# Moving the MLP input and the low weights of narrow pieces to other SBUF remainders

## The chip, the cores and the metric

The kernel runs on one core of one Trainium2 chip. The metric is the device time of one execution in microseconds (us); the kernel before takes 1369.39 us (median of 3 runs, 1369.24 to 1369.44).

## The reference, cut to what matters

A trunk of four decoder layers works on one sequence of 256 tokens with 1024 features in float32. Each layer adds a token mixer (retention, block-sparse attention, differential attention, retention again) and then an MLP:

```python
for i in range(DEPTH):
    h = _rmsnorm(x, norm1[i])
    x = x + mixer_i(h)
    u = relu(_rmsnorm(x, norm2[i]) @ w_up[i])      # 1024 -> 4096
    x = x + (u * u) @ w_down[i]                    # 4096 -> 1024
```

Some 237 MB of weights are read once each.

## The kernel before, in words

**Split products.** Every large product is made of float32r matmuls. An operand is split into a high part (a copy rounded to float32r, made by ScalarE) and a low part (operand minus high part, made by VectorE), and `passes` (L296 to L299) issues three matmuls into one PSUM bank: high times high (L297), high times low (L298), low times high (L299). The weight load of the next matmul runs on TensorE beside the stream of the present one.

**Weights.** `load_raw` fetches 1 MB at a time from SyncE's queue into one of three `raw` buffers. `split_piece` takes half of it and makes `whi` (L164), `split_lo` makes `wlo` (L174) and asks for the next load once both halves of a buffer are split. Six buffers of 4 KB a partition exist for each of `whi` and `wlo`, and `advance` keeps up to five pieces ahead of the one in use.

**Three shapes of piece.** A piece of `spec_a` (4 x 256 elements) is called narrow: `mm_a` uses it, with 128 columns of the weights as the stationary operand and 256 columns of the activations (`xhi`, `xlo`) as the moving one. They serve the MLP's up product (tile `up`) and retention's q and k (tile `qk`). Pieces of `spec_b` (2 x 512) and `spec_o` (1 x 1024) are wide: in `mm_b` (tiles `vg`, `qkv`) and `mm_o` (tile `acc`) the weights are the moving operand, 512 columns at a time, and the activations are the stationary one: `xhi`, `xlo` in `mm_b`; `uu` (the MLP's hidden values, high and low) or `oh`, `ol` (the mixer's output) in `mm_o`.

**What a narrow group does.** For each of 4 row blocks `passes(ps, whi, wlo, xhi, xlo)` runs. L297 moves `xhi` against `whi`, while `whi` is loaded a second time for L298. L298 moves `xlo`, while `wlo` is loaded for L299. L299 moves `xhi`, while the next `whi` is loaded for the next block's L297.

**Order.** The order of TensorE's work is written out by hand. In the MLP a step is `up(s + 1)` (two narrow pieces, 48 matmuls) and then two `out_piece` calls (24 wide matmuls); there are 16 steps in a layer. Small work (norms, softmax, transposes) is put between by `later` and `tick`.

**Normalised input.** `norm_new` allocates `xhi` and `xlo` (8 KB a partition each), once for the mixer's input and once for the MLP's input of every layer; `finish` calls it, and `norm_quarter` fills the two tiles.

**Where the tiles lie.** Pools lie one behind the other, in the order `const`, `op`, `xp`, `up`, `wp`, `mp`, `rp`. `xp` holds `xhi` and then `xlo`; `up` holds six buffers of 4 KB (`uu`, `vh`, `vl` and others); `wp` holds six `whi` and then six `wlo`. All of these sizes are multiples of 1024 bytes, so in the kernel before all of them have one remainder modulo 1024. Retention's scores `s` (high and low) lie in `mp`, behind five small tiles of three buffers padded to 32 bytes each, so they start 480 bytes off that remainder.

Of the kernel before, what the change touches and what calls it, by code (L numbers as in the profile page):

```python
# [10 lines left out]
F32R = mybir.dt.float32r  # L11
# [5 lines left out]
P = 128  # L17
S = 256
# [3 lines left out]
KC = D // P  # L22
# [9 lines left out]
def trunk(ctx, tc, x_in, rel_bias, norm1, norm2, w_up, w_down, ret_w_in, ret_w_out,  # L32
# [9 lines left out]
    xp = ctx.enter_context(tc.tile_pool(name="xp", bufs=1))  # L42
    up_ = ctx.enter_context(tc.tile_pool(name="up", bufs=1))
    wp = ctx.enter_context(tc.tile_pool(name="wp", bufs=1))
# [7 lines left out]
    NRAW, NPC = 3, 6  # L52
# [13 lines left out]
    def later(n, fn, *a):  # L66
        clock[1] += 1
        pending.append((clock[0] + n, ORDER.get(fn.__name__, 3), clock[1], fn, a))
# [10 lines left out]
    def tick():  # L79
        clock[0] += 1  # L80
        run_due()


    specs = []

    def ap2(w, off, dims):
# [62 lines left out]
    def parts(i, n):  # L149
        m = n if i else n // 2  # L150
        return [slice(c, c + m) for c in range(0, n, m)]

    def split_piece():
        i = nxt[1]
        r = i // 2
        if r >= len(specs):
            return
        nxt[1] += 1
        _, a, b = specs[r]
        half = raws[r][:, (i % 2) * (a // 2):(i % 2 + 1) * (a // 2), :]  # L160
        hi = wp.tile([P, a // 2, b], F32R, tag="hi", name="whi", bufs=NPC)
        lo = wp.tile([P, a // 2, b], F32R, tag="lo", name="wlo", bufs=NPC)
        for part in parts(i, a // 2):
            ACT.activation(hi[:, part], half[:, part], AF.Copy)  # L164
        pieces[i] = (hi, lo, half)
# [13 lines left out]
    def advance(ah=4, al=4):  # L179
        while True:  # L180
            a, b = nxt[1], nxt[3]
            if nxt[1] <= nxt[2] + ah and nxt[1] // 2 < len(specs):
                split_piece()
            if nxt[3] <= nxt[2] + al:
                split_lo()
            if (a, b) == (nxt[1], nxt[3]):
                return

    def take():
        p = pieces.pop(nxt[2])  # L190
        nxt[2] += 1
        return p
# [66 lines left out]

    st = {}  # L260

    def norm_new():
        st["hi"] = xp.tile([P, KC, S], F32R, tag="xhi", name="xhi")
        st["lo"] = xp.tile([P, KC, S], F32R, tag="xlo", name="xlo")

    def norm_quarter(l, which, c, t):
        tt = slice(t * P, (t + 1) * P)
# [65 lines left out]
    def mm_o(q, piece, src, first, last):  # L333
        c, t = q
        hi, lo = piece
        uh, ul = src
        tt = slice(t * P, (t + 1) * P)
        cc = slice(c * 512, (c + 1) * 512)
        passes(st["acc"][q], uh[:, tt], ul[:, tt], hi[:, 0, cc], lo[:, 0, cc], first, last)
# [8 lines left out]
    def finish(srcs, r2, nxt_norm):  # L348
        advance(4, 4)
        pcs = [take() for _ in srcs]  # L350
        if nxt_norm is not None:
            norm_new()
        for q in QUARTERS:
            for i, (pc, src) in enumerate(zip(pcs, srcs)):
                mm_o(q, pc, src, False, i == len(srcs) - 1)
            c, t = q
            xs = X[:, t, c * 512:(c + 1) * 512]
            ps = st["acc"][q]
            if r2 is None:
                DVE.tensor_tensor(xs, ps, xs, op=OP.add)  # L360
            else:
                DVE.scalar_tensor_tensor(xs, ps, r2[:, t:t + 1], xs, op0=OP.mult, op1=OP.add)
            if nxt_norm is None:
                nc.sync.dma_start(out.rearrange("b s d -> (b s) d")[t * P:(t + 1) * P, c * 512:(c + 1) * 512], xs)
            else:
                later(2, norm_quarter, nxt_norm[0], nxt_norm[1], c, t)
            tick()
        if nxt_norm is not None:
            later(3, rms, nxt_norm[1])


    def mlp(l):
# [21 lines left out]
        for s in range(16):  # L394
            if s + 1 < 16:
                up(s + 1)
            if not acc:
                acc_new()
                acc = True
            if s < 14:  # L400
                for m in range(2):
                    out_piece(U[s][m], s == 0 and m == 0)
                del U[s]
            elif s == 14:
                out_piece(U[s][0], False)
            else:
                finish([U[14][1]] + U[15], st["r2"], (l + 1, 0) if l + 1 < DEPTH else None)


    def retention(l):  # L410
# [107 lines left out]
        for c in range(13):  # L518
            h, i = divmod(c, 4)
            out_piece((OT[h][0][:, i, :], OT[h][1][:, i, :]), c == 0)  # L520
        finish([(OT[3][0][:, i, :], OT[3][1][:, i, :]) for i in (1, 2, 3)], None, (l, 1))


# [33 lines left out]
    def attention(l):  # L557
# [193 lines left out]
        for c in range(5):  # L751
            out_piece(srcs[c], c == 0)
        finish(srcs[5:], None, (l, 1))


    norm_new()
    for t in range(2):
        norm_quarter(0, 0, 0, t)
    split_piece()
    split_lo()  # L760
    for t in range(2):
        later(1, norm_quarter, 0, 0, 1, t)
    later(1, split_piece)
    later(1, split_lo)
    later(3, rms, 0)
# [50 lines left out]
```

## Time and profile before

| | |
|---|---|
| median of 3 runs | 1369.39 us |
| the profiled execution, its own time | 1369.67 us |
| its span, first to last instruction | 1367.9 us |
| TensorE (PE) matmul busy | 1351.8 us (99%) |
| weight loads (PEld) busy | 1188.7 us (87%) |
| VectorE (DVE), ScalarE (ACT), GpSimd (POOL) busy | 61%, 50%, 8% |
| weights' DMA queue, share of 16 engines | 51.5% |

The busy time of an engine counts overlapping instructions once. A matmul's duration is its time from start to the modelled end, longer than the distance to the next matmul's start, since matmuls are pipelined; the time of the kernel goes by the distance between starts. In the windows of one engine alone only that engine's busy time stands. In groups of lines a row reads: line, engine, operation, output and inputs, shapes and count, then busy us and the mean duration in ns, then idle time before.

### The profile page before, as it was taken

How to read it: one execution, taken by the hardware profiler on the slowest of the kernel's cores; microseconds unless marked ns; L12 is line 12 of the kernel's file. 1: busy time of each engine (PE TensorE's matmuls, PEld its weight loads, DVE VectorE, ACT ScalarE, POOL GpSimd, SP SyncE). 2: the span in 40 equal slices, each digit the busy share in tenths (PEclk: the TensorE clock that was granted, in tenths of full speed). 3: DMA queues.
4: the chain of work that ended last, by engine and by line, in shares of the span. 5: the costliest groups of instructions: out<-in, count | busy, mean ns of one | idle time of the engine just before them, and what ended most of it. 6: DMA issues, size and time to landing. Idle time of an engine off the chain costs nothing.

```text
span 1367.9 us, 19806 instructions
## 1 busy us (share of the span) xinstructions
PE 1351.8 (99%) x8020; PEld 1188.7 (87%) x8020; DVE 840.8 (61%) x1238; ACT 689.7 (50%) x1063; POOL 107.1 (8%) x314
## 2 busy tenths in 40 slices
PE   7999999999999999999999999999999999999998
PEld 7888889999987779999987789999988888899997
DVE  6766647555568856555578675555667675555554
ACT  5554436444456745444466754444454444544442
POOL 3111100000032000000021200000031011000000
PEclk9999999999999999999999999999999999999999
DMA  8545464555565346555554346555564555465551
GB/s 274 184 155 184 156 214 157 187 187 188 193 206 181 123 124 219 185 185 185 184 172 137 124 154 216 185 185 185 176 206 144 174 185 185 154 215 186 185 184 63
DMA packets 140797, 242.27 MB, mean 177 GB/s; under 512 B 4256, under 2 KB 87920, under 8 KB 140704
## 3 DMA queue, kind: packets, MB, share of 16 engines
q1 hardware_dynamic: 137872, 236.99, 51.5%
q0 software_dynamic: 1072, 2.35, 0.6%
q10 hardware_dynamic: 1760, 1.66, 0.4%
q8 instruction: 63, 1.03, 0.3%
q14 instruction: 30, 0.25, 0.1%
HBM read 239.91 MB, written 1.07 MB: 176 GB/s over the span
## 4 chain that ended last, share of the span: by engine, by line
PE 97%; ACT 1%; DMA 0%; DVE 0%; issue 0%; SPq 0%; ACTq 0%; DVEq 0%
PE acc L297 12%; PE acc L298 12%; PE acc L299 12%; PE up L299 9%; PE up L298 9%; PE up L297 9%; PE vg L297 4%; PE vg L299 4%; PE vg L298 4%; PE qkv L297 3%; PE qkv L299 3%; PE qkv L298 3%; PE qk L299 2%; PE qk L297 2%; PE qk L298 2%; PE xt L272 1%
## 5 line engine op out<-in xcount | busy, mean ns | idle before, releaser
L174 DVE TENSOR_TENSOR wlo<-raw,whi 128x1024 fp32r<-128x1024 f32 (+1 forms) x449 | 529.5, 1219 | 108.1 <-ACT whi L164 105.8
L164 ACT ACTIVATE whi<-raw 128x1024 fp32r<-128x1024 f32 (+1 forms) x449 | 451.9, 1051 | 90.8 <-PE acc L299 66.8
L297 PE MATMUL up<-xhi,whi 128*128 128x256 f32 x1024 | 290.1, 283 | 0.0
L299 PE MATMUL up<-xhi,wlo 128*128 128x256 f32 x1024 | 289.8, 283 | 0.0
L298 PE MATMUL up<-xlo,whi 128*128 128x256 f32 x1024 | 289.7, 283 | 0.0
L297 PE MATMUL acc<-whi,uu 128*128 128x512 f32 x512 | 200.5, 392 | 0.0
L298 PE MATMUL acc<-wlo,uu 128*128 128x512 f32 x512 | 199.9, 390 | 0.0
L299 PE MATMUL acc<-whi,uu 128*128 128x512 f32 x512 | 199.3, 389 | 0.0
L298 PEld LDWEIGHTS up<-xlo,whi 128*128 128x128 f32 x1024 | 196.3, 192 | 2.2
L297 PEld LDWEIGHTS up<-xhi,whi 128*128 128x128 f32 x1024 | 196.3, 192 | 2.2
L299 PEld LDWEIGHTS up<-xhi,wlo 128*128 128x128 f32 x1024 | 196.3, 192 | 0.0
L378 DVE SCALAR_TENSOR_TENSOR u<-up,u 128x512 f32<-128x512 f32 x64 | 44.2, 691 | 221.7 <-ACT u L377 221.5
L377 ACT ACTIVATE u<-up 128x512 f32<-128x512 f32 x64 | 38.1, 596 | 258.9 <-PE up L299 258.9
L299 PEld LDWEIGHTS acc<-whi,uu 128*128 128x128 f32 x512 | 96.1, 188 | 20.5
L297 PEld LDWEIGHTS acc<-whi,uu 128*128 128x128 f32 x512 | 96.4, 188 | 18.2
L298 PEld LDWEIGHTS acc<-wlo,uu 128*128 128x128 f32 x512 | 96.4, 188 | 17.6
L297 PE MATMUL vg<-whi,xhi 128*128 128x512 f32 x256 | 100.6, 393 | 0.0
L299 PE MATMUL vg<-whi,xlo 128*128 128x512 f32 x256 | 99.8, 390 | 0.0
L298 PE MATMUL vg<-wlo,xhi 128*128 128x512 f32 x256 | 99.7, 390 | 0.0
L297 PE MATMUL qkv<-whi,xhi 128*128 128x512 f32 x192 | 78.0, 406 | 0.0
L297 PE MATMUL acc<-whi,oh 128*128 128x512 f32 x192 | 76.4, 398 | 0.0
L297 PE MATMUL qk<-xhi,whi 128*128 128x256 f32 x256 | 74.0, 289 | 1.8 <-ACT whi L164 1.8
(212 smaller groups left out, 1807.7 us busy)
## 6 DMA issues: line engine op xcount, KB each, us to landing
raw<-in_w_up_dram SPq DMA_DIRECT2D x64, 1024.0 KB, 5.5
raw<-in_w_down_dram SPq DMA_DIRECT2D x64, 1024.0 KB, 5.9
raw<-in_ret_w_in_dram SPq DMA_DIRECT2D x47, 1024.0 KB, 5.2
raw<-in_ret_w_out_dram SPq DMA_DIRECT2D x16, 1024.0 KB, 4.9
raw<-in_moba_w_in_dram SPq DMA_DIRECT2D x12, 1024.0 KB, 5.2
raw<-in_diff_w_in_dram SPq DMA_DIRECT2D x12, 1024.0 KB, 5.1
raw<-in_moba_w_out_dram SPq DMA_DIRECT2D x4, 1024.0 KB, 4.8
raw<-in_diff_w_out_dram SPq DMA_DIRECT2D x4, 1024.0 KB, 4.7
```

What stands on the lines that cost most here:

```text
L164: ACT.activation(hi[:, part], half[:, part], AF.Copy)
L174: DVE.tensor_tensor(lo[:, part], half[:, part], hi[:, part].bitcast(F32), op=OP.subtract)
L272: PE.transpose(ps[:, i * P:(i + 1) * P], X[:, t, k * P:(k + 1) * P], ident)
L297: PE.matmul(ps, lhsT=ah, rhs=bh, start=first, stop=False, skip_group_check=True)
L298: PE.matmul(ps, lhsT=ah, rhs=bl, start=False, stop=False, skip_group_check=True)
L299: PE.matmul(ps, lhsT=al, rhs=bh, start=False, stop=last, skip_group_check=True)
L377: ACT.activation(u, ps, AF.Relu)
L378: DVE.scalar_tensor_tensor(u, ps, 0.0, u, op0=OP.max, op1=OP.mult)
```

## The change

Only addresses are changed. `wlo` gets a tag of its own for each of six places, padded by 128 bytes (odd places) or 384 bytes (even places), and the tile starts inside that padding or not, depending on place and shape. `xhi` and `xlo` are padded by 320 and 192 bytes, `xlo` is allocated first, and the MLP's input starts at other offsets in them than the mixer's input. Instructions, their order, shapes, DMAs and waits stay.

```diff
+    def hi_lo(i, a, b, narrow):
+        n = a * b
+        hi = wp.tile([P, n], F32R, tag="hi", name="whi", bufs=NPC)
+        odd = i % 2
+        lo = wp.tile([P, n + (32 if odd else 96)], F32R, tag="lo%d" % (i % NPC), name="wlo", bufs=1)
+        o = 0 if odd == narrow else (32 if odd else 96)
+        return (t.rearrange("p (a b) -> p a b", a=a) for t in (hi, lo[:, o:o + n]))
...
-        hi = wp.tile([P, a // 2, b], F32R, tag="hi", name="whi", bufs=NPC)
-        lo = wp.tile([P, a // 2, b], F32R, tag="lo", name="wlo", bufs=NPC)
+        hi, lo = hi_lo(i, a // 2, b, a == 8)
...
-    def norm_new():
-        st["hi"] = xp.tile([P, KC, S], F32R, tag="xhi", name="xhi")
-        st["lo"] = xp.tile([P, KC, S], F32R, tag="xlo", name="xlo")
+    def norm_new(mlp_in=False):
+
+        n = KC * S
+        lo = xp.tile([P, n + 48], F32R, tag="xlo", name="xlo")
+        hi = xp.tile([P, n + 80], F32R, tag="xhi", name="xhi")
+        oh, ol = (64, 48) if mlp_in else (80, 0)
+        st["hi"] = hi[:, oh:oh + n].rearrange("p (k s) -> p k s", k=KC)
+        st["lo"] = lo[:, ol:ol + n].rearrange("p (k s) -> p k s", k=KC)
...
-            norm_new()
+            norm_new(nxt_norm[1] == 1)
```

Worked out from these sizes, the starts in bytes, counted from the start of `whi` and modulo 1024, are:

| tile | before | after |
|---|---|---|
| `whi`, `uu`, `vh`, `vl` | 0 | 0 |
| `wlo`, narrow piece | 0 | 384 or 896 |
| `wlo`, wide piece | 0 | 0 or 512 |
| mixer input `xhi`, `xlo` | 0, 0 | 0, 512 |
| MLP input `xhi`, `xlo` | 0, 0 | 960, 704 |
| `oh`, `ol` | 0 | 512 |
| `s` | 480 | 992 |

The slices that are used within a tile begin at multiples of 512 bytes in both kernels. So modulo 512 everything that was at 0 stays there, except for the narrow `wlo` (384) and the MLP's `xhi` (448) and `xlo` (192); `s` stays at 480.

## Rows read from the trace of the kernel before

**Rows 1.** The page: busy time of engines; granted clock by slice of the span.

```profile
PE 1351.8 (99%) x8020; PEld 1188.7 (87%) x8020; DVE 840.8 (61%) x1238; ACT 689.7 (50%) x1063; POOL 107.1 (8%) x314
...
PEclk9999999999999999999999999999999999999999
```

**Rows 2.** The page: the chain that ended last, by engine.

```profile
PE 97%; ACT 1%; DMA 0%; DVE 0%; issue 0%; SPq 0%; ACTq 0%; DVEq 0%
```

**Rows 3.** Groups of lines, shapes apart: narrow and wide matmuls.

```profile
L297 PE MATMUL up<-xhi,whi 128*128 128x256 f32 x1024 | 290.1, 283 | 0.0
L299 PE MATMUL up<-xhi,wlo 128*128 128x256 f32 x1024 | 289.8, 283 | 0.0
L298 PE MATMUL up<-xlo,whi 128*128 128x256 f32 x1024 | 289.7, 283 | 0.0
...
L298 PE MATMUL acc<-wlo,uu 128*128 128x512 f32 x512 | 199.9, 390 | 0.0
...
L298 PE MATMUL qk<-xlo,whi 128*128 128x256 f32 x256 | 73.0, 285 | 0.0
```

**Rows 4.** Timeline, TensorE, one MLP step: start us, duration us, instruction.

```profile
300.27 0.40 PE L297 MATMUL acc<-whi,uu 128*128 128x512 f32 x1
...
301.43 0.39 PE L299 MATMUL acc<-whi,uu 128*128 128x512 f32 x1
...
305.51 0.39 PE L299 MATMUL acc<-whi,uu 128*128 128x512 f32 x1
305.74 0.28 PE L297 MATMUL up<-xhi,whi 128*128 128x256 f32 x1
305.85 0.28 PE L298 MATMUL up<-xlo,whi 128*128 128x256 f32 x1
...
311.37 0.28 PE L299 MATMUL up<-xhi,wlo 128*128 128x256 f32 x1
```

**Rows 5.** Tile up, 306.2 to 311.3 us: duration ns min/median/max, first and last start.

```profile
L299 PE MATMUL up<-xhi,wlo x15: 283/283/283, 306.0 to 311.0; 128*128 128x256 f32 x15
L297 PE MATMUL up<-xhi,whi x15: 283/283/283, 306.1 to 311.1; 128*128 128x256 f32 x15
```

**Rows 6.** Line L481, transposes of retention: duration ns min/median/max.

```profile
L481 PE MATMUL oT<-ident,go x64: 270/272/273, 56.8 to 1143.9; 128*128 128x128 f32 x64
```

**Rows 7.** Tile up, whole run: duration ns min/median/max.

```profile
L297 PE MATMUL up<-xhi,whi x1024: 277/283/364, 209.6 to 1352.2; 128*128 128x256 f32 x171
L298 PE MATMUL up<-xlo,whi x1024: 278/283/283, 209.8 to 1352.3; 128*128 128x256 f32 x171
```

**Rows 8.** Tiles vg and o, whole run: duration ns min/median/max.

```profile
L298 PE MATMUL vg<-wlo,xhi x256: 387/389/398, 25.6 to 1137.2; 128*128 128x512 f32 x128
...
L298 PE MATMUL o<-vl,s x24: 393/396/397, 41.0 to 1129.0; 128*128 128x512 f32 x24
```

**Rows 9.** Timeline, TensorE, retention's score product between two `vg` groups.

```profile
77.51 0.39 PE L299 MATMUL vg<-whi,xlo 128*128 128x512 f32 x1
...
78.19 0.40 PE L299 MATMUL vg<-whi,xlo 128*128 128x512 f32 x1
78.42 0.39 PE L297 MATMUL o<-vh,s 128*128 128x512 f32 x1
...
80.52 0.39 PE L297 MATMUL vg<-whi,xhi 128*128 128x512 f32 x1
...
81.20 0.39 PE L297 MATMUL vg<-whi,xhi 128*128 128x512 f32 x1
```

**Rows 10.** Groups of weight loads, shapes apart: busy us, mean ns.

```profile
L298 PEld LDWEIGHTS up<-xlo,whi 128*128 128x128 f32 x1024 | 196.3, 192 | 2.2
...
L298 PEld LDWEIGHTS acc<-wlo,uu 128*128 128x128 f32 x512 | 96.4, 188 | 17.6
```

**Rows 11.** Windows, one MLP's up phase and one narrow run: us, busy by engine; PEclk, DMA share, GB/s.

```profile
209.63:378.97 169.34, 169.34 (x1112) 155.84 (x1111) 96.65 (x102) 83.02 (x104) 1.27 (x3) 1.00 0.56 191
...
305.85:311.37 5.52, 5.52 (x48) 1.00 0.80 249
```

**Rows 12.** Waits of SyncE's queue: us in total, times, longest.

```profile
SPq L142 <- DVE wlo L174: 1172.4, 216, 16.1
```

## The prediction

> **What bounds the kernel now.** I read the page's busy times first: matmuls cover 99% of the span, VectorE 61%, ScalarE 50%, and the granted clock is at full speed, the 2.4 GHz level, in all slices [rows 1]. The chain that ended last is 97% TensorE with no DMA in it [rows 2]. So the time is the number of matmuls times the distance between their starts, and a change of addresses can matter only through that distance. Then the groups of lines: 3072 narrow matmuls belong to the MLP's up product, 1024 for each of the three passes, 283 ns each; the wide ones take some 390 ns [rows 3]. Since durations overlap, I took distances from the timeline. In a narrow run 46 distances fill the 5.52 us from 305.85 to 311.37, which is 120.0 ns each; between the wide ones 18 distances fill the 4.08 us from 301.43 to 305.51, which is 226.7 ns [rows 4].
>
> **There is something to gain in it.** At 2.4 GHz 256 columns stream in 106.7 ns and 512 in 213.3 ns. Both shapes take 13.3 ns more than that. The excess lies inside the matmul: 30 matmuls in a row lasted 283 ns to the nanosecond [rows 5], while a transpose, which also streams for 106.7 ns (128 columns of float32 in two cycles each, an estimate from its duration), lasts 272 ns [rows 6]. The difference, 11 ns, is a stretch of the stream while the next weights are loaded. Two readings tell that the stretch isn't fixed. First, the earliest narrow matmul after a wide group starts 0.11 us before the next one, not 0.12 [rows 4], and matmuls of the very same form have lasted as little as 277 or 278 ns [rows 7]. Second, an address moves it: in retention's score product the stationary operand `s` lies 480 bytes off the common remainder (32 below it modulo 512), and there the wide matmul lasts 396 ns where that of `vg` lasts 389 [rows 8]. The timeline shows it coming and going: three distances in 0.68 us before, 227 ns each; ten in 2.33 us, 233 ns each, of which nine load `s`; and three in 0.68 us again behind it [rows 9]. So remainders of the two operands that are read at once count, by +6.3 ns in the one case that can be seen.
>
> **Part by part.** The pair that counts is the stream and the weights loaded beside it. Call distance the start of the weights less that of the stream, modulo 512. Before, it is 0 in all three passes of a narrow group. After, in the MLP, L297 (moves `xhi`, loads `whi`) has 0 - 448 = 64; L298 (moves `xlo`, loads `wlo`) 384 - 192 = 192; L299 (moves `xhi`, loads the next `whi`) 64.
>
> (1) The 3072 narrow matmuls of the MLP. No row shows a distance of 64 or 192, so this is bounded. Best: the whole stretch goes, 283 to 272 [rows 5, 6], 11 ns x 3072 = 33.8 us less. Worst: they behave as `s` does, 6.3 ns more [rows 9], 19.4 us more. I take 6 ns less, from 283 to the 277 that the same form of instruction reaches in this kernel [rows 7], which is also near the distance of 0.11 us behind that short matmul [rows 4]: it is the nearest row, the same operation at another phase between stream and load, where the transposes are another operation and `s` another shape. 6 ns x 3072 = **18.4 us less**.
>
> (2) Retention's `qk`: of its 768 matmuls only the 256 of L298 change (stream at 0, weights at 384); the other two passes keep 0. Bounds as above: 256 x 11 = 2.8 us less to 256 x 6.3 = 1.6 us more; I take 0, its own row's 285 ns [rows 3], since two neighbours of three stay as they are.
>
> (3) Wide matmuls: `wlo`, `oh`, `ol` and the mixer's `xlo` shift by 0 or 512 against the rest. Slices at both steps occur before too, as every second stationary slice begins 512 bytes on, and the median stays 389 [rows 8]. Cost 0, unless modulo 512 isn't the rule (last rival).
>
> (4) The seam. Behind each narrow run five wide matmuls take 1.16 us (300.27 to 301.43) instead of 5 x 226.7 = 1133 ns [rows 4], 27 ns extra; 16 runs in each of four layers make 1.7 us. It could vanish or double; I take no change, ends 1.7 us on each side.
>
> (5) The engines that write the shifted tiles. VectorE is busy for 96.65 and ScalarE for 83.02 of the 169.34 us of an up phase [rows 11]; with 768 x 6 ns = 4.6 us less it is 59% and 50%, so slower writes stay hidden. Weights: 191 GB/s would have to become 191 x 169.34 / 164.7 = 196, and a narrow run already shows 249 [rows 11]. SyncE's queue waits 1172 us for `wlo` to free a buffer [rows 12], so loads are early, not late. No instruction, wait or DMA is added or moved. Cost 0.
>
> Sum against the profiled execution: 1369.67 - 18.4 = 1351.3 us. It lies 0.3 us above the median of 1369.39, so I forecast **1351 us**.
>
> **Rivals.** *The shift does nothing* (20%): 1369 us. For it: only an offset of 32 bytes has been seen to act, and a shift by 512 did nothing; all of the new distances are multiples of 64 bytes, so if what counts is a place within a small line, the pairs look as before. Against it: the stretch depends on phase, and a shift of 64 bytes is some 7 ns of the stream, a change of phase. The Trainium skill would have it so too: TensorE: Matmul & The Clock Gate, Part 2 (the step on LDWEIGHTS), says that TensorE reads moving operand and weights through two independent ports, so that loading the next weights takes nothing from the running matmul. By that rule no remainder matters and the sum would be 0. The trace speaks against it here: 396 ns against 389 with `s` [rows 8].
>
> *Weight loads set the pace* (12%): in the up phase they are busy for 155.84 of 169.34 us [rows 11], and a load lasts 192 ns beside narrow matmuls, 188 beside wide ones [rows 10]. If a narrow matmul cannot start until its load is through, only the 4 ns by which loads are held up come back: 4 x 3072 = 12.3 us, 1357 us. The spacing of 0.11 us speaks against it.
>
> *The new distances collide more* (18%): the stream reads two bytes where the load reads one (120 ns for 1024 bytes, beside 512 bytes of weights), so a stream that begins 64 bytes behind its weights runs into them early, where at distance 0 it starts level and leaves them behind. With the stretch of `s` on all three passes it is 19.4 us more, 1389 us; on L298 alone, 1024 x 6.3 = 6.5 us more, 1376 us. It decides as soon as the mean stretch of the three passes is over 11 ns. In it I count that the wide operands don't keep one remainder as the change says: the MLP's 1536 wide matmuls alone (512 a pass [rows 3]) x 6.3 = 9.7 us, 1379 us.
>
> **How the numbers follow.** 50% for the forecast (gains from 6 to 34 us), 12% for loads that set the pace, together 62% faster; 20% for no effect; 18% slower. About 0.2% (2.7 us) is what a measurement of this kernel can tell from no change. The range goes from the whole stretch, 1369.4 - 33.8 = 1336, to one pass in three worsened, 1376; beyond the upper end are the cases with two or three passes worsened, some 13%.
>
> **What would show it.** Right: `up` rows at 272 to 278 ns instead of 283 in all three lines, up phases of about 164.7 us instead of 169.34, wide rows at 389 and 390 as before, `s` as before. If only L298 or only L297 and L299 get shorter, one distance works and the other doesn't. The forecast is wrong if `up` stays at 283 (no effect), if loads show 188 and `up` about 279 (pace of the loads), if `up` is over 283 (collision), or if gaps of TensorE that wait for `wlo` or `raw` appear, which would say that the cover in (5) is gone.

## The result, and the profile after

The changed kernel takes 1352.09 us (median of 4 runs, 1349.88 to 1353.06) against 1369.41 us of the kernel before, a ratio of 0.9865 (95% interval 0.9853 to 0.9877): 17.3 us less, where 18.4 were forecast. Its profiled execution took 1352.26 us with a span of 1350.4 us, 17.4 and 17.5 us less than that of before.

The page's busy times and chain, and the groups of the matmuls that the terms of the sum name (the lines of `passes` are L311 to L313 now):

```profile
PE 1333.6 (99%) x8020; PEld 1170.5 (87%) x8020; DVE 840.6 (62%) x1238; ACT 689.3 (51%) x1063; POOL 106.6 (8%) x314
...
PE 97%; ACT 1%; DMA 1%; DVE 0%; issue 0%; SPq 0%; ACTq 0%; DVEq 0%
...
L311 PE MATMUL up<-xhi,whi 128*128 128x256 f32 x1024 | 283.8, 277 | 0.0
L312 PE MATMUL up<-xlo,whi 128*128 128x256 f32 x1024 | 283.5, 277 | 0.0
L313 PE MATMUL up<-xhi,wlo 128*128 128x256 f32 x1024 | 283.2, 277 | 0.0
...
L312 PE MATMUL acc<-wlo,uu 128*128 128x512 f32 x512 | 199.6, 390 | 0.0
```

```profile
L313 PEld LDWEIGHTS up<-xhi,wlo 128*128 128x128 f32 x1024 | 192.5, 188 | 0.0
```

The kernel is bound as before. `up` is shorter, from 283 to 277 ns in all three passes, its weight loads last 188 ns instead of 192 [rows 10], and the wide `acc` keeps its 390 ns [rows 3]. By tile, `up` sits at its minimum: 276 ns is now both the least and the median, where 277 was the exception and 283 the rule [rows 7]; `qk` spreads around 282:

```profile
L312 PE MATMUL up<-xlo,whi x1024: 276/276/284, 209.7 to 1334.8; 128*128 128x256 f32 x171
...
L312 PE MATMUL qk<-xlo,whi x256: 278/282/415, 9.6 to 1099.3; 128*128 128x256 f32 x128
...
L312 PE MATMUL vg<-wlo,xhi x256: 387/389/398, 25.8 to 1124.4; 128*128 128x512 f32 x128
...
L312 PE MATMUL o<-vl,s x24: 393/396/397, 41.2 to 1116.2; 128*128 128x512 f32 x24
```

The timeline of one narrow run gives the distances, to be read against [rows 4]:

```profile
302.81 0.39 PE L313 MATMUL acc<-whi,uu 128*128 128x512 f32 x1
303.04 0.28 PE L311 MATMUL up<-xhi,whi 128*128 128x256 f32 x1
...
303.86 0.28 PE L312 MATMUL up<-xlo,whi 128*128 128x256 f32 x1
...
308.39 0.28 PE L313 MATMUL up<-xhi,wlo 128*128 128x256 f32 x1
308.51 0.39 PE L311 MATMUL acc<-whi,uu 128*128 128x512 f32 x1
...
309.66 0.39 PE L313 MATMUL acc<-whi,uu 128*128 128x512 f32 x1
```

The last 40 distances of the run fill 4.53 us, 113.3 ns each instead of 120.0. The first seven fill 0.82 us, 117 ns each: a run needs some eight matmuls to settle. Behind it five wide ones take 1.15 us instead of 1.16. The windows, with columns as in [rows 11], show where the time went and where some came back:

```profile
209.54:374.24 164.70, 164.70 (x1112) 151.31 (x1111) 96.65 (x102) 82.97 (x104) 1.27 (x3) 1.00 0.58 195
503.57:668.27 164.70, 164.70 (x1112) 151.31 (x1111) 96.64 (x102) 82.98 (x104) 0.80 (x2) 1.00 0.58 195
...
668.26:798.15 129.89, 126.70 (x645) 101.98 (x644) 93.30 (x239) 81.36 (x197) 24.96 (x86) 0.99 0.43 143
```

An up phase takes 164.70 us, 4.64 less than before [rows 11]; four of them give 18.6 us. The stretch between the second and the third one, the differential attention, took 128.39 us before and takes 129.89 now:

```profile
677.65:806.04 128.39, 125.19 (x645) 100.81 (x644) 93.32 (x239) 81.44 (x197) 25.05 (x86) 1.00 0.43 144
```

So 1.5 us come back there, and the granted clock of 0.99 tells why. The window that holds it and the 10 us ahead of it, and the same two in a second profile of the changed kernel (x10 below):

```profile
748.00:758.00 10.00, 7.53 (x47) 5.07 (x47) 5.06 (x28) 8.21 (x36) 3.48 (x18) 1.00 0.23 91
757.90:761.50 3.60, 3.60 (x9) 2.81 (x10) 3.46 (x17) 3.49 (x10) 0.78 (x3) 0.53 0.02 5
```

```profile
748.00:758.00 10.00, 7.53 (x46) 5.14 (x46) 5.17 (x28) 8.24 (x36) 3.48 (x18) 1.00 0.23 90
757.90:761.50 3.60, 3.60 (x17) 2.90 (x17) 3.46 (x15) 3.59 (x10) 0.78 (x3) 1.00 0.02 5
```

In the first of these two profiles, TensorE's clock is at its lower level (1.2 GHz) for nearly all of these 3.6 us, and 9 matmuls fall in the window instead of 17. Ahead of it the engine had been busy for 7.53 of 10 us, waiting for softmax work; in the second profile it had been just as busy, and the clock stayed. The profiles of x4 (its window here) and x11 below have the same drop at the same work, and those of x2, x3, x9 and x12 have none:

```profile
763.90:767.50 3.60, 3.60 (x11) 2.77 (x10) 3.46 (x13) 3.30 (x9) 0.78 (x3) 0.53 0.00 0
```

So the drop does not come with the change. With it the sum of the profiled execution closes: 18.6 less in up phases, 0.3 less in the second retention layer (207.98 to 207.67 us between up phases), 0.1 before the first, 1.5 more here, 17.5 in all; without the drop it would be 19.0. Of ten later executions of the kernel before, three took 1369.4 to 1369.5 us at a mean granted clock of 0.999 or more and seven 1370.5 to 1371.2 us at 0.998, so that a comparison moves by about 1.5 us with the share of such drops on either side.

### The profile page after: what moved, and what is told of

Same layout as the page of the kernel before. It is cut to its first block, busy times and chain, and to the rows that moved or that the text cites. A ratio compares the mean times of both kernels' runs of the same rounds, so it can differ in the third digit from the quotient of the medians.

```text
span 1350.4 us, 19806 instructions
## 1 busy us (share of the span) xinstructions
PE 1333.6 (99%) x8020; PEld 1170.5 (87%) x8020; DVE 840.6 (62%) x1238; ACT 689.3 (51%) x1063; POOL 106.6 (8%) x314
## 4 chain that ended last, share of the span: by engine, by line
PE 97%; ACT 1%; DMA 1%; DVE 0%; issue 0%; SPq 0%; ACTq 0%; DVEq 0%
PE acc L311 12%; PE acc L312 12%; PE acc L313 12%; PE up L312 9%; PE up L313 9%; PE up L311 9%; PE vg L311 4%; PE vg L313 4%; PE vg L312 4%; PE qkv L311 3%; PE qkv L313 3%; PE qkv L312 3%; PE qk L313 2%; PE qk L311 2%; PE qk L312 2%; PE xt L286 1%
## 5 line engine op out<-in xcount | busy, mean ns | idle before, releaser
L311 PE MATMUL up<-xhi,whi 128*128 128x256 f32 x1024 | 283.8, 277 | 0.0
L312 PE MATMUL up<-xlo,whi 128*128 128x256 f32 x1024 | 283.5, 277 | 0.0
L313 PE MATMUL up<-xhi,wlo 128*128 128x256 f32 x1024 | 283.2, 277 | 0.0
L311 PE MATMUL acc<-whi,uu 128*128 128x512 f32 x512 | 199.9, 391 | 0.0
L313 PE MATMUL acc<-whi,uu 128*128 128x512 f32 x512 | 199.5, 390 | 0.0
L312 PEld LDWEIGHTS up<-xlo,whi 128*128 128x128 f32 x1024 | 192.3, 188 | 2.2
L311 PEld LDWEIGHTS up<-xhi,whi 128*128 128x128 f32 x1024 | 192.2, 188 | 2.2
L313 PEld LDWEIGHTS up<-xhi,wlo 128*128 128x128 f32 x1024 | 192.5, 188 | 0.0
L313 PEld LDWEIGHTS acc<-whi,uu 128*128 128x128 f32 x512 | 96.1, 188 | 20.2
L311 PEld LDWEIGHTS acc<-whi,uu 128*128 128x128 f32 x512 | 96.1, 188 | 17.8
L311 PE MATMUL vg<-whi,xhi 128*128 128x512 f32 x256 | 100.5, 393 | 0.0
L313 PE MATMUL vg<-whi,xlo 128*128 128x512 f32 x256 | 99.8, 390 | 0.0
L311 PE MATMUL qkv<-whi,xhi 128*128 128x512 f32 x192 | 78.6, 409 | 0.0
L311 PE MATMUL acc<-whi,oh 128*128 128x512 f32 x192 | 76.5, 398 | 0.0
L313 PE MATMUL qkv<-whi,xlo 128*128 128x512 f32 x192 | 75.7, 394 | 0.0
```

The source lines that it names most:

```text
L311: PE.matmul(ps, lhsT=ah, rhs=bh, start=first, stop=False, skip_group_check=True)
L312: PE.matmul(ps, lhsT=ah, rhs=bl, start=False, stop=False, skip_group_check=True)
L313: PE.matmul(ps, lhsT=al, rhs=bh, start=False, stop=last, skip_group_check=True)
```

## The experiments

Theory A is the prediction's: each pass goes by its own pair, the stream and the weights loaded beside it, and by their distance modulo 512. Theory B says that the tiles must lie at different remainders. Theory C says that the weight loads set the pace. Theory D came out of the first four runs: the three passes act on each other.

Below, a triple (low weights, high stream, low stream) gives starts modulo 256 counted from the high weights. The MLP's narrow product is (0, 0, 0) before and (128, 192, 192) after, since 384, 448 and 192 are that modulo 256; retention's `qk` is (128, 0, 0) after.

**x1, one distance at a time.** The core of the kernel:

```python
def run(name, d, cols, n):
    ps = pp.tile([P, 512], F32, tag="ps", name=name, bufs=8)
    for i in range(n):
        PE.matmul(ps[:, :cols], lhsT=sta[:, d // 4:d // 4 + P], rhs=mov[:, :cols],
                  start=i == 0, stop=i == n - 1, skip_group_check=True)
```

> Leaves the trunk out: the output is a copy of x, and TensorE runs groups of 24 equal matmuls, each with weights that start d bytes off the stream (d = 0 to 992 in steps of 32; 256 columns twice, then 512 columns). If the distance between stream and weights sets the stretch (theory A), 256 columns last 283 ns at d = 0 and 512, 276 or 277 ns at 64, 576, 192 and 704, and 512 columns last 389 ns at 0 and 512 and 394 to 396 ns at 480 and 992. If the rule is that the tiles lie at different remainders of their own (theory B), or if the pace is that of the weight loads alone (theory C), all groups of one width last the same.

The groups of lines (n is 256 columns, w 512, then the distance in bytes):

```profile
L53 PE MATMUL n0000x<-mov,sta 128*128 128x256 f32 x48 | 6.1, 283 | 0.0
L53 PE MATMUL n0256x<-mov,sta 128*128 128x256 f32 x48 | 6.1, 282 | 0.0
...
L53 PE MATMUL n0064x<-mov,sta 128*128 128x256 f32 x48 | 6.0, 281 | 0.0
...
L53 PE MATMUL n0192x<-mov,sta 128*128 128x256 f32 x48 | 6.0, 279 | 0.0
...
L53 PE MATMUL w0064x<-mov,sta 128*128 128x512 f32 x24 | 5.8, 396 | 0.0
...
L53 PE MATMUL w0480x<-mov,sta 128*128 128x512 f32 x24 | 5.8, 395 | 0.0
...
L53 PE MATMUL w0000x<-mov,sta 128*128 128x512 f32 x24 | 5.7, 391 | 0.0
...
L53 PE MATMUL w0256x<-mov,sta 128*128 128x512 f32 x24 | 5.6, 389 | 0.0
```

The weight loads of three of these groups:

```profile
L53 PEld LDWEIGHTS n0000x<-mov,sta 128*128 128x128 f32 x48 | 5.9, 191 | 0.0
...
L53 PEld LDWEIGHTS n0160x<-mov,sta 128*128 128x128 f32 x48 | 5.9, 188 | 0.0
...
L53 PEld LDWEIGHTS w0000x<-mov,sta 128*128 128x128 f32 x24 | 4.4, 188 | 0.9
```

The distance counts, so theories B and C are out as they stand. But the period is 256 bytes, not 512: 256, 512 and 768 are all like 0. And theory A's 276 or 277 ns at 64 and 192 are missed: with one distance throughout they last 281 and 279 ns, with starts 117.8 ns apart for both, while the changed kernel shows 276 ns with a mixture of the two. For 512 columns 0 is the best of all, with 256 and its multiples.

**x2 to x4, parts of the change.** Against the changed kernel, x2 has `wlo` unshifted, x3 has the tiles of `norm_new` as before, and x4 moves the two low parts together; their edits in that order:

```diff
-        lo = wp.tile([P, n + (32 if odd else 96)], F32R, tag="lo%d" % (i % NPC), name="wlo", bufs=1)
-        o = 0 if odd == narrow else (32 if odd else 96)
+        lo = wp.tile([P, n], F32R, tag="lo", name="wlo", bufs=NPC)
```

```diff
-        st["hi"] = hi[:, oh:oh + n].rearrange("p (k s) -> p k s", k=KC)
-        st["lo"] = lo[:, ol:ol + n].rearrange("p (k s) -> p k s", k=KC)
+        st["hi"] = xp.tile([P, KC, S], F32R, tag="xhi", name="xhi")
+        st["lo"] = xp.tile([P, KC, S], F32R, tag="xlo", name="xlo")
```

```diff
-        lo = xp.tile([P, n + 48], F32R, tag="xlo", name="xlo")
-        hi = xp.tile([P, n + 80], F32R, tag="xhi", name="xhi")
-        oh, ol = (64, 48) if mlp_in else (80, 0)
+        lo = xp.tile([P, n + 96], F32R, tag="xlo", name="xlo")
+        hi = xp.tile([P, n + 32], F32R, tag="xhi", name="xhi")
+        oh, ol = (32, 96) if mlp_in else (32, 0)
```

> Only the MLP input is shifted; wlo is as before. Distances: L297 64, L298 320 (512 - 192), L299 64. Theory A: two of three passes keep the whole gain (277 ns), L298 is open between 277 and 283; 1351 to 1358 us. Theory B: wlo and whi share a remainder again, so some of the gain of the passes that load either goes, and the three passes lose it alike.

> Only the narrow wlo is shifted (384); the MLP input is as before. Distances: L297 0, L298 384, L299 0, as in retention's qk after the change. Theory A: up as qk is after the change, 281 to 282 ns instead of 283 and distances of 117 to 121 ns, so 1364 to 1369 us. Theory B: a third of the gain at least, 1363 us or less.

> The MLP's xlo and the narrow wlo both lie at 384, xhi and whi both at 0: other remainders for the low parts, yet distance 0 in all three passes. Theory A: 283 ns, distances of 120 ns, 1369 us as before. Theory B (different remainders are what helps): at least the pass that reads low parts is shortened, 1363 us or less.

Measured: x2 1361.33 us (ratio 0.9936, 0.9919 to 0.9952, to 1370.74 before on that chip), x3 1366.55 us (0.9976, 0.9965 to 0.9987), x4 1363.10 us (0.9947, 0.9932 to 0.9962). Their rows by tile, in that order: the low stream's pass of each, and for x4 the third pass too:

```profile
L310 PE MATMUL up<-xlo,whi x1024: 276/281/282, 209.7 to 1343.8; 128*128 128x256 f32 x171
```

```profile
L308 PE MATMUL up<-xlo,whi x1024: 278/283/287, 209.5 to 1349.1; 128*128 128x256 f32 x171
```

```profile
L312 PE MATMUL up<-xlo,whi x1024: 278/282/282, 209.2 to 1346.2; 128*128 128x256 f32 x171
L313 PE MATMUL up<-xhi,wlo x1024: 277/280/285, 209.3 to 1346.4; 128*128 128x256 f32 x171
```

x3 lies where theory A had it. x2 misses theory A: two passes have the distances of the change, yet all three have a median of 281 ns and none settles at 276. x4 refutes it: all three distances are 0, which theory A prices at 283 ns, and the passes last 280 to 282. Theory B fits the even loss of x2 and the time of x4 (1363.10 us, of 1363 or less), but not x1, and not x3, where it had 1363 us or less. And 9.4 us (x2) and 4.2 us (x3) make 13.6, not the whole: the two shifts are worth more together than one by one. So the passes act on each other.

**x5 and x6, the map of all triples.** The core; a triple has a group of its own, in steps of 32 bytes, 512 groups for each width:

```python
for i in range(blocks):
    for st, so, mv, mo in ((hw, 0, hm, bh), (hw, 0, lm, bl), (lw, al, hm, bh)):
        PE.matmul(ps[:, :cols], lhsT=st[:, so // 4:so // 4 + P], rhs=mv[:, mo // 4:mo // 4 + cols], ...)
```

> Leaves the trunk out: groups of 30 matmuls of 256 columns in the order of the three passes (high weights and high stream, high weights and low stream, low weights and high stream), one group for each triple of starts modulo 256 in steps of 32, taken from the high weights: low weights, high stream, low stream. If each pass goes by its own pair alone (theory A), a group lasts the mean of three values of the first sweep, no shorter than 117.2 ns a matmul, and the triple of the change (128, 192, 192) 117.7 ns. If the three passes act on each other (theory D), that triple lasts 113.3 ns, (0, 192, 192) 117.7, (128, 0, 128) about 117, (128, 0, 0) about 119, and other triples lie on both sides, possibly at the 109 ns of an unstretched stream.

> The same with 512 columns, groups of 27 matmuls. Triple (0, 0, 0) 226.7 ns as in the kernel. Theory A: nothing is shorter than 226.7, since that was the shortest of the first sweep, and most lie at 233. Theory D: some triple may reach 220 ns, one step of 6.7 ns less, which would be worth 3456 times 6.7, 23 us, in the kernel.

By tile (l, h, m: low weights, high stream, low stream), the first pass of four triples of x5, and then the second pass of two of x6:

```profile
L56 PE MATMUL nl128h192m192x<-bh,ah x10: 276/276/283, 1125.4 to 1128.5; 128*128 128x256 f32 x10
...
L56 PE MATMUL nl000h192m192x<-bh,ah x10: 281/281/283, 217.8 to 221.0; 128*128 128x256 f32 x10
...
L56 PE MATMUL nl128h000m128x<-bh,ah x10: 274/280/282, 947.7 to 950.8; 128*128 128x256 f32 x10
...
L56 PE MATMUL nl128h000m000x<-bh,ah x10: 278/282/285, 933.5 to 936.7; 128*128 128x256 f32 x10
```

```profile
L56 PE MATMUL wl000h000m000x<-bl,ah x9: 389/389/389, 39.2 to 44.6; 128*128 128x512 f32 x9
...
L56 PE MATMUL wl000h192m192x<-bl,ah x9: 393/398/398, 377.1 to 382.7; 128*128 128x512 f32 x9
```

Nothing but TensorE works beside these groups: VectorE has no instruction on the page, and the 6 of ScalarE come ahead of them. So the stretch needs no other engine's reads or writes:

```profile
PE 1832.7 (99%) x15480; PEld 1832.5 (99%) x15480; ACT 5.3 (0%) x6; POOL 0.2 (0%) x4
```

From the starts of the last 12 to 15 distances of each group, means in ns:

| triple | where it occurs | 256 columns |
|---|---|---|
| (0, 0, 0) | before | 120.0 |
| (128, 192, 192) | `up` after | 113.3 |
| (0, 192, 192) | x2 | 117.8 |
| (128, 0, 0) | x3; `qk` after | 119.1 |
| (128, 0, 128) | x4 | 117.8 |
| mean, best, second best, worst of 512 | | 118.2, 113.3, 115.5, 122.3 |

Theory D holds, and with it the parts come out: an up phase has 768 narrow matmuls, so x2 should have 169.34 - 768 x 2.2 ns = 167.65 us, x3 168.65 and x4 167.65. The windows of their first up phases show 167.41, 168.73 and 167.67. The triple of the change is the best of all 512, by 2.2 ns, and its six neighbours, 32 bytes away in one tile, all lie at about 117.8 ns. A group has only 30 matmuls, so a triple that settles later than that would not show its best. For 512 columns (0, 0, 0) is the best of the map at 226.7 ns, shared with (128, 0, 160), where the mean is 232.1 and the worst 236.7. No triple reaches 220.

**x7 and x8, finer steps and another order.** The same groups with other triples; an order is a list of passes (weights, stream; 0 high, 1 low):

```python
A = ((0, 0), (0, 1), (1, 0))
B = ((0, 0), (1, 0), (0, 1))
```

> Leaves the trunk out: 640 further triples for 256 columns, in steps of 16 bytes with at least one odd multiple of 16, and 64 triples in steps of 64 with the order of the second and third pass exchanged. If 113.3 ns at (128, 192, 192) is the end of what a place can give, nothing is below 113; if a finer place takes the rest of the stretch away, some triple is between 109 and 113 ns.

> The same for 512 columns, 448 triples. If (0, 0, 0) is the best place for wide operands, nothing is below 226.7 ns; a triple at 220 ns would be worth 23 us in the kernel.

Nothing falls below 113.3 or 226.7 ns among the 640 and 448 finer triples sampled or the 64 of each width with the order exchanged. Three more of the finer triples settle at 113.3 ns, (128, 16, 16), (32, 144, 96) and (32, 64, 16), two at 226.7 for 512 columns, (16, 0, 240) and (144, 192, 112), and with the order exchanged (0, 192, 192) does as well as (128, 192, 192). The 109 ns from start to start that the transposes of the kernel show were not found.

**x9, the weights moved instead of the input; x10, the change again.**

```diff
+        hi = wp.tile([P, n + 64], F32R, tag="hi", name="whi", bufs=NPC)
+        lo = wp.tile([P, n + 64], F32R, tag="lo", name="wlo", bufs=NPC)
+        oh, ol = (16, 48) if narrow else (0, 0)
+        return (t.rearrange("p (a b) -> p a b", a=a) for t in (hi[:, oh:oh + n], lo[:, ol:ol + n]))
...
-        oh, ol = (64, 48) if mlp_in else (80, 0)
+        st["hi"] = xp.tile([P, KC, S], F32R, tag="xhi", name="xhi")
+        st["lo"] = xp.tile([P, KC, S], F32R, tag="xlo", name="xlo")
```

> The activations stay where they were before the change; instead the narrow whi lies 64 bytes and the narrow wlo 192 bytes behind the common remainder. Counted from whi that is the triple (128, 192, 192) again, modulo 256, and now for retention's qk as well. If only the places of the four tiles against each other count, up and qk both go to 113.3 ns: up as after the change, qk from 119.1 to 113.3, 768 times 5.8, 4.5 us below the changed kernel, 1347.6 us. If the MLP input's own remainder counts, up stays at 118 to 120 ns and the time is 1360 us or more.

> The changed kernel itself, beside the other on the same chip: 1350 us where the clock stays at its full level all through, some 2 us more where it falls to the lower level for 3.4 us in the differential attention.

x9 takes 1346.63 us (1346.19 to 1348.31), ratio 0.9827 (0.9813 to 0.9842) to 1370.80 before; x10 1351.03 us (1350.32 to 1351.68), 0.9858 (0.9842 to 0.9875). By tile, x9 has both products at 276 ns:

```profile
L307 PE MATMUL up<-xlo,whi x1024: 276/276/283, 207.6 to 1329.1; 128*128 128x256 f32 x171
...
L307 PE MATMUL qk<-xlo,whi x256: 276/276/416, 9.4 to 1093.6; 128*128 128x256 f32 x128
```

So the input's own remainder does not count, and the places of the four tiles against each other, modulo 256, are enough for this triple (x11 shows that it is not so for every one). x9 beats both kernels, the changed one by 4.4 us in the medians and 4.1 in the profiled executions (1346.45 against 1350.52), where 768 x 5.8 ns are 4.5, since retention's `qk` joins without the mixer's input leaving the place that its wide use needs.

**x11, another of the best triples.**

```diff
-        oh, ol = (16, 48) if narrow else (0, 0)
+        oh, ol = (60, 28) if narrow else (0, 0)
```

> The narrow whi lies 240 and the narrow wlo 112 bytes behind the common remainder, activations as before the change: the triple (128, 16, 16) of the finer map, also 113.3 ns. up and qk last 276 ns again. If only the settled value counts, the time is that of x9, 1346.6 us; in the map this triple settled sooner (113.97 ns over the whole group against 115.0), which over 80 narrow runs of 48 matmuls could be 1 to 2 us less.

A miss: 1365.14 us, ratio 0.9960 (0.9947 to 0.9974).

```profile
L306 PE MATMUL up<-xhi,whi x1024: 276/279/364, 209.1 to 1347.8; 128*128 128x256 f32 x171
L307 PE MATMUL up<-xlo,whi x1024: 277/282/289, 209.3 to 1347.9; 128*128 128x256 f32 x171
```

The run never settles at 276 ns. Two things differ from the map: the high weights begin at another place within 32 bytes, since here the weights and not the streams are 16 off, and the run is entered from wide matmuls. Which of them it is was not tried. The last 12 distances of its runs have a mean of 118.1 or 118.2 ns. The triples of the changed kernel, x2, x3 and x4 are entered from wide matmuls too and have there what the map has (113.3, 117.8, 119.3 and 117.8 ns); that speaks against the entry, but does not decide it.

**x12, the other half of the change's rule.** The kernel before with `uu` moved:

```diff
-            uu = up_.tile([P, 4, S], F32R, tag="p4k", name="uu", bufs=6)
+            uu = up_.tile([P, 4 * S + 64], F32R, tag="p4k", name="uu", bufs=6)
+            uu = uu[:, 16:16 + 4 * S].rearrange("p (m s) -> p m s", m=4)
```

> The kernel before, with only uu, the stationary operand of the MLP's 1536 wide matmuls, 64 bytes off the common remainder; nothing narrow is changed. From the wide map, triple (0, 192, 192): 233.3 to 233.5 ns instead of 226.7, 1536 times 6.7, 10 us slower than before, 1379 to 1381 us. If wide operands need no common remainder, 1370 us.

1377.32 us (1377.02 to 1378.53) against 1370.72, ratio 1.0052 (1.0038 to 1.0065): 6.6 us slower, of 10 expected.

```profile
L298 PE MATMUL acc<-wlo,uu x512: 392/394/398, 221.7 to 1370.4; 128*128 128x512 f32 x171
...
L299 PE MATMUL up<-xhi,wlo x1024: 278/283/283, 209.7 to 1359.5; 128*128 128x256 f32 x171
```

The wide matmuls of the MLP are stretched, in the pass shown to a median of 394 ns from the 389 of before:

```profile
L298 PE MATMUL acc<-wlo,uu x512: 387/389/398, 222.0 to 1363.0; 128*128 128x512 f32 x171
```

The price was set against the settled 226.7 ns, while the five unsettled ones behind each narrow run cost some 27 ns more before as well [rows 4]; 64 x 27 ns are 1.7 of the 3.4 us that are missing. Another 1.1 are in the narrow runs: from the first start to that of the wide ones behind, a run of 48 took 5.75 us before and takes 5.73 here, 17.5 ns less, 64 times. An up phase is 1.7 us longer than before [rows 11], 6.8 us in four:

```profile
209.35:380.38 171.03, 171.03 (x1112) 155.66 (x1111) 96.62 (x102) 82.97 (x104) 1.27 (x3) 1.00 0.56 189
```

## Why the prediction was right, and where it was not

The forecast (faster, 1351 us) and its bound held: the kernel is TensorE from end to end, the stretch of the stream is not fixed, addresses move it, and no instruction was added.

*Step (1)*, 18.4 us for the MLP's narrow matmuls, measured 18.6 in the up phases (4 x 4.64). The price of 6 ns, taken from the 277 ns that the same form had reached, was near the settled 6.7 ns; 768 x 6.7 are 5.1 us a phase, of which some 0.6 are lost in the settling at the head of each run, which the sum did not have, and 0.2 come back behind it (step 4). The upper bound, the 272 ns of a transpose, is not to be had by any of the places tried.

*The working behind it was wrong in two points.* "The pair that counts is the stream and the weights loaded beside it": the pair is not enough. x4 has all pairs at 0 and still differs from before, and a constant 64 or 192 gives 281 and 279 ns where their mixture gives 276. All four tiles count at once, as the map shows; by what mechanism their reads act on each other, no run shows. And "modulo 512" is modulo 256 (x1). Both would have misled a search: by pairs, x2 should have kept two thirds of the gain, and it has 9.4 of some 19 us (17.3 in the first comparison, 19.8 in x10).

So the size of step (1) is in part luck. In the kernel before, the 277 ns belong to the first matmul of a run, behind a wide one (277 or 278 ns in all of 56 runs of 48), and not to a distance of 64 or 192. By the prediction's own rule, with the 117.8 ns that x1 measured for both distances, the sum would have been 3072 x 2.2 ns, 6.8 us less, some 1363 us; the rest comes from all places acting together, which the prediction did not have.

*Step (2)*, retention's `qk` at no cost: right in size, 0.3 us less in the second layer; its triple (128, 0, 0) is 0.9 ns better than before, not neutral. *Step (3)*, wide operands unchanged: right, and x12 shows what it would have cost otherwise. *Step (4)*, the seam: 1.15 us against 1.16, about 12 ns less behind each run, 0.8 us in all, where no change was taken. *Step (5)*: VectorE is busy for 96.65 us of an up phase as before, and the weights come at 195 GB/s, where 196 were worked out.

*The rivals.* That the shift does nothing fell; so did the rule of the Trainium skill behind it (TensorE: Matmul & The Clock Gate, Part 2, the step on LDWEIGHTS), that loading the next weights takes nothing from the running matmul: in x1 the same 512-column matmul lasts 389 or 396 ns by where its weights lie. Loads as the pace fell too. Its sign was loads of 188 ns and `up` at about 279; the loads do last 188 ns now, but `up` lasts 277 and gains more than the 4 ns of the loads. In x1 at a distance of 160 the loads last 188 ns, and the starts of the matmuls are still 120.0 ns apart. The collision rival named the wrong place (a small positive distance), but the danger is real: all other wide triples of the map but one are slower than (0, 0, 0), and at the worst narrow ones, (192, 0, 224) and (32, 128, 192) with 122.2 to 122.3 ns, `up` would have been 3072 x 2.3 ns, 7 us, slower than before.

What the forecast lacked besides is the drop of the granted clock in the differential attention, 1.5 us of the profiled execution, which some executions of either kernel seem to have.

## What to carry to other kernels

For float32r matmuls with a weight load each, as here: where TensorE is busy for 99% and a matmul's distance to the next is above columns divided by the clock, compare the starts of the moving and stationary tiles modulo 256 bytes before touching the schedule. Measure the places of all operands of the repeating pattern together, in a small kernel that runs every combination; tuning one operand at a time would have found half of it here at best (9.4 us in x2, 4.2 in x3). If operands serve two patterns with different best places, move the operand that belongs to one pattern alone (x9), and check the result in the kernel itself, as a triple that is best in the map need not settle there (x11).

## What the runs showed that was not expected

At one common remainder the distances, 120.0 and 226.7 ns, are 106.7 and 213.3 plus the same 13.3, and the best narrow one, 113.3, lies one half of that lower; most triples settle at neither (117.8 in x2, 119.1 in x3). At the lower clock level no stretch is seen: between 758.18 and 761.17 us of the changed kernel seven distances of 512 columns fill 2.99 us, 427 ns each, which is 512 columns at 1.2 GHz and nothing more.

```profile
758.18 0.63 PE L312 MATMUL qkv<-wlo,xhi 128*128 128x512 f32 x1
...
761.17 0.52 PE L313 MATMUL qkv<-whi,xlo 128*128 128x512 f32 x1
```
